# Moving operands 256 bytes behind the stationary ones, and gates built from 2-byte tables two tokens at a time

## The chip, the cores and the metric

The kernel runs on one core of one Trainium2 chip. The metric is the device time of one execution in microseconds (us). Before the change it is 2248.18 us, the median of 3 runs (2247.75 to 2248.98).

## The reference, cut to what matters

256 tokens of width 1024 pass through two blocks. The first is a gated MLP with a spatial mix, then attention with a sliding window. The second is retention, then latent attention, and behind each of these two stands a PEER layer. All matrix products are float32. The PEER layer is where the second half of the change works:

```python
def peer_ffn(x, w_q, sub_keys, u, v):
    ...
        s1, i1 = lax.top_k(s[:, :, 0], PEER_TOPK)
        s2, i2 = lax.top_k(s[:, :, 1], PEER_TOPK)
        ...
        top_s, pos = lax.top_k(cand_s, PEER_TOPK)
        eidx = jnp.take_along_axis(cand_i, pos, axis=-1)
        gate = jax.nn.softmax(top_s, axis=-1).astype(xb.dtype)
        h = jax.nn.gelu(jnp.einsum('thkd,td->thk', u[eidx], xb), approximate=False)
        return jnp.einsum('thk,thkd->td', gate * h, v[eidx])
```

Each token picks 8 heads x 16 experts out of 128 x 128 = 16384, and each picked expert is one neuron with a row of u, a row of v and a gate.

## The kernel before

A float32 product is made of three products of a rounded type (fp32r). ScalarE rounds an operand to its high part (line 155), VectorE subtracts to get the low part (line 156), and TensorE adds up high x high, high x low and low x high (lines 164, 165, 166). Weights come in units of 128 x 1024 floats (512 KB, `unit`, line 118), each cut into two pieces of 512 columns, `wh` and `wl`.

There are two ways to multiply. In `o2` (line 271) the weight piece is the stationary operand (128 columns at a time) and the tokens `xh`, `xl` are the moving one, 256 columns wide; one unit is 24 matmuls. It serves the gates of the MLP, of the attention and of retention, part of the queries, and the 128 units of u in each PEER layer. In `o1_unit` and `out_unit` the tokens are stationary and 512 columns of weights move; one unit of v is 12 matmuls.

Where the operands lie in a partition of SBUF: `front` begins with a pad of `X_PAD` floats (lines 37 and 52), then come `xh` and `xl`; the tile of `eps` is drawn out to `EPS_ROOM` floats (lines 36 and 57), so that what follows begins at a chosen place within 512 bytes. In this layout every `wh` and `wl` begins 160 bytes behind a multiple of 512, and `xh` and `xl` begin 352 bytes behind one: the moving operand of an `o2` matmul begins 192 bytes behind the stationary one, counted within 512. `apart` (line 175) does the same for the other token tiles that move (`xg`, `cqT`, `ckT`), with `APART` floats. In a unit of v the weights move and the other operand (`wdh`, `wdl`) also begins at 160, so there the distance is 0. Where the tokens `xh` are stationary and weights move (line 164 with `mm<-wh,xh`), it is 160 - 352, that is 320 within 512.

The PEER layer does not gather rows. It computes h for all 16384 experts (`u_block`, 128 units), multiplies it with a gate that is zero for the experts that were not picked, and runs all of v (`v_block`, 128 units). The gates come 8 tokens (`NT`) and 64 blocks of experts (`nb`) at a time from `gates` (line 1186): a one-hot `a` of 128 columns for each of the 128 picks of a token (its second index), a one-hot `e` of 64 columns (its first index), `b` as `e` times the high and the low part of the gate's weight, and two matmuls of 64 columns for each token, `a` stationary, `b` moving: 16 matmuls. VectorE compares `iota` (float32) with a table of indices (float32). For 6 of 8 groups ScalarE makes `a` instead, with one Square for each token and one Relu for four tokens (lines 1198 and 1199). The gate is multiplied into h in place by one instruction on VectorE that reads PSUM (line 1148).

Two passes of 32 gates run in each layer, woven (`weave`, line 104) one gate to two units: pass 1 between the last 64 units of u, pass 2 between the first 62 units of v. Behind pass 2 come the other units of v without gates. Each engine works through its own queue in the order that the program gives.

Of the kernel before, what the change touches and what calls it, by code (L numbers as in the profile page):

```python
# [10 lines left out]
F32 = mybir.dt.float32  # L11
F32R = mybir.dt.float32r
F16 = mybir.dt.float16
BF16 = mybir.dt.bfloat16
I32 = mybir.dt.int32
U32 = mybir.dt.uint32
AF = mybir.ActivationFunctionType
ALU = mybir.AluOpType
# [12 lines left out]
NPEER = 2  # L31
NBEGIN = 3
U2 = 64
PASSES = ((0, 64, 64, 6), (64, 64, 62, 6))
NT = 8
LINE = 512
EPS_ROOM = 48
X_PAD = 56
APART = 48
END_PAD = 80  # L40
GSCALE = 2.0 ** 15

# [1 line left out]
class Net:  # L44
    def __init__(s, ctx, tc, aps):
# [10 lines left out]
        s.cp = ctx.enter_context(tc.tile_pool(name="consts", bufs=1))  # L56
        s.eps = s.cp.tile([128, EPS_ROOM], F32, name="eps")[:, 0:1]

# [116 lines left out]
    def apart(pool, shapes):  # L175

        pool.tile([128, APART], F32, name="gap")
        tiles = [pool.tile(shape, F32R, name=name) for shape, name in shapes]
# [901 lines left out]
    def peer(s, i, outs, begin):  # L1080
        nc, d = s.nc, s.d
        with ExitStack() as es:


            p = pw = es.enter_context(s.pool(f"pw{i}", "right"))
            s.more_weights(es, f"wp{i}", 0, NPEER, "right")
            pg = es.enter_context(s.pool(f"pg{i}"))
            X = (s.xh, s.xl)
            tabs = [pw.tile([128, 256], F32, name=f"tab{j}") for j in range(2)]
            tabs.append(pw.tile([128, 2, 256], F16, name="tabg"))  # L1090
            hst = [es.enter_context(s.pool(f"ph{i}")).tile([128, 64, 256], F32, name="h0")]

            routing = ExitStack()
            skv = routing.enter_context(s.pool(f"ps{i}", "right")).tile([128, 2048], F32, name="sk")
            with s.urgent():
                nc.sync.dma_start(skv, d[f"p_sk{i}"])
            pk = routing.enter_context(s.pool(f"pk{i}", "right"))
            scratch = pk.tile([128, 2, 28 * 128], F32, name="scratch")
            q4 = pk.tile([128, 2, 512], F32, name="q4")
            si = pk.tile([128, 2, 2, 16, 16], F32, name="si")  # L1100
            rest = pk.tile([128, 256], F32, name="rest")
            s16 = [si[:, t, 0] for t in range(2)]
            i16 = [si[:, t, 1].bitcast(U32) for t in range(2)]

            def row(b):
                return hst[b // 64][:, b % 64, :]

            def u_block(b):
                hp = s.mm("acc")
                s.o2(s.unit(d[f"p_u{i}"][b]), 0, KB, X, hp[:, :256])  # L1110
                nc.scalar.activation(row(b), hp[:, :256], AF.Gelu)  # L1111

            qs = {}

            def q_unit(c):
                if c < 4:
                    qp = s.transposes(lambda j: q4[:, j, c * 128:c * 128 + 128], 2)
                else:
                    qp = s.mm()
                    s.o2(s.unit(d[f"p_q{i}"][c]), 0, KB, X, qp[:, :256])  # L1120
                qs[c] = p.tile([128, 256], F32, name="qT", tag="wd", bufs=6)
                nc.scalar.copy(qs[c], qp[:, :256])

            def s_unit(c):
                qT, sk = qs.pop(c), skv[:, c * 128:c * 128 + 128]
                sc = s.mm()
                for tt in range(2):
                    o = sc[:, tt * 128:tt * 128 + 128]
                    nc.tensor.matmul(o, qT[:, tt * 128:tt * 128 + 128], sk, start=True, stop=True)
                ss = p.tile([128, 256], F32, name="ss", tag="wd", bufs=6)  # L1130
                nc.scalar.copy(ss, sc[:, :256])
                for tt in range(2):
                    s.top16(rest[:, tt * 128:tt * 128 + 128], s16[tt][:, c, :], i16[tt][:, c, :],
                            ss[:, tt * 128:tt * 128 + 128])

            def v_in(b):
                wh = p.tile([128, 256], F32R, name="wdh", tag="wd", bufs=6)
                wl = p.tile([128, 256], F32R, name="wdl", tag="wd", bufs=6)
                s.split(wh, wl, row(b))
                return wh, wl  # L1140

            def v_block(b):
                s.out_unit(acc, s.unit(d[f"p_v{i}"][b]), v_in(b), False, False)

            def gate(t0, b0, nb, act):
                gp = s.gates(pg, t0, b0, nb, tabs, t0 // NT * act % 8 < act)
                hv = hst[b0 // 64][:, b0 % 64:b0 % 64 + nb, t0:t0 + NT].rearrange("p b t -> p t b")
                nc.vector.scalar_tensor_tensor(hv, gp[:, :NT * nb].rearrange("p (t b) -> p t b", b=nb),  # L1148
                                               1.0 / (GSCALE * ALPHA), hv,
                                               op0=ALU.mult, op1=ALU.mult)  # L1150

            for tt in range(2):
                nc.scalar.copy(q4[:, tt, :], outs[tt])
            for c in range(16):
                q_unit(c)
                u_block(c)
                s_unit(c)
            steps = []
            for tt in range(2):
                i16f = si[:, tt, 1]  # L1160
                nc.vector.tensor_copy(i16f, i16[tt])
                g = s.route(s16[tt], i16f, scratch[:, tt])
                steps += [lambda g=g: next(g)] * 16
            steps.append(lambda: s.gate_tables(scratch, tabs))
            s.weave([lambda b=b: u_block(b) for b in range(16, U2)], steps)
            routing.close()
            hst.append(es.enter_context(s.pool(f"pv{i}", "right")).tile([128, 64, 256], F32, name="h1"))
            blocks = [lambda b=b: u_block(b) for b in range(U2, 128)]
            for b0, nb, n, act in PASSES:
                s.weave(blocks[:n], [lambda t=t: gate(t, b0, nb, act) for t in range(0, 256, NT)])  # L1170
                blocks = blocks[n:]
                if b0 == 0:
                    for f in blocks:
                        f()
                    acc = s.accs()
                    s.skip_path(acc)
                    blocks = [lambda b=b: v_block(b) for b in range(125)]
            s.warm(hst[1][:, 63, 0:1])
            for f in blocks:
                f()  # L1180
            s.finish(acc, [d[f"p_v{i}"][b] for b in (125, 126, 127)], [v_in(b) for b in (125, 126, 127)])
            room = [hst[1][:, 36 + 4 * j:40 + 4 * j, :].rearrange("p b t -> p (b t)") for j in range(4)]

            return s.hand_over(s.post_ln(room, acc, d["ln_ffn_g"][i], d["ln_ffn_b"][i]), begin)

    def gates(s, p, t0, b0, nb, tabs, act):

        nc = s.nc
        i1t, i2t, gt = tabs
        sl = slice(t0, t0 + NT)  # L1190
        a = p.tile([128, NT, 128], F16, name="ga", tag="ga", bufs=2)
        if act:

            for j0 in range(0, NT, 4):
                q = p.tile([128, 4, 128], BF16, name="gq", tag="gq", bufs=1)
                for j in range(4):
                    t = t0 + j0 + j
                    nc.scalar.activation(q[:, j, :], s.iota, AF.Square, scale=-1.0, bias=i2t[:, t:t + 1])  # L1198
                nc.scalar.activation(a[:, j0:j0 + 4, :], q, AF.Relu, scale=-1.0, bias=1.0)  # L1199
        else:  # L1200
            nc.vector.tensor_tensor(a, s.iota[:, None, :].to_broadcast([128, NT, 128]),
                                    i2t[:, sl, None].to_broadcast([128, NT, 128]), op=ALU.is_equal)
        e = p.tile([128, NT, nb], F16, name="ge1", tag="g3", bufs=2)
        nc.vector.tensor_tensor(e, s.iota[:, None, b0:b0 + nb].to_broadcast([128, NT, nb]),  # L1204
                                i1t[:, sl, None].to_broadcast([128, NT, nb]), op=ALU.is_equal)
        b = p.tile([128, 2, NT, nb], F16, name="gb", tag="g2", bufs=2)
        nc.vector.tensor_tensor(b, e[:, None].to_broadcast([128, 2, NT, nb]),  # L1207
                                gt[:, :, sl, None].to_broadcast([128, 2, NT, nb]), op=ALU.mult)
        gp = s.mm()
        for j in range(NT):  # L1210
            for k in range(2):
                nc.tensor.matmul(gp[:, j * nb:(j + 1) * nb], a[:, j, :], b[:, k, j, :], start=k == 0, stop=k == 1)  # L1212
        return gp


# [97 lines left out]
```

## Time and profile before

| what | value |
|---|---|
| median of 3 runs | 2248.18 us |
| the profiled execution | 2246.99 us |
| its span, first to last instruction | 2245.3 us |
| TensorE, share of the span with a matmul in flight | 98% |
| VectorE | 83% |
| ScalarE | 68% |
| DMA, mean busy share | 53% |

TensorE's row counts a matmul as busy until its modelled end, and the next one begins long before that. So 98% does not say that TensorE runs at its best pace; the pace is read from the starts of successive matmuls in the timeline. The shares are means over stages with different limits: in the units of v without gates VectorE is a third idle, in pass 2 it is busy all the time.

### The profile page before, as it was taken

How to read it: one execution, taken by the hardware profiler on the slowest of the kernel's cores; microseconds unless marked ns; L12 is line 12 of the kernel's file. 1: busy time of each engine (PE TensorE's matmuls, PEld its weight loads, DVE VectorE, ACT ScalarE, POOL GpSimd, SP SyncE). 2: the span in 40 equal slices, each digit the busy share in tenths (PEclk: the TensorE clock that was granted, in tenths of full speed). 3: DMA queues.
4: the chain of work that ended last, by engine and by line, in shares of the span. 5: the costliest groups of instructions: out<-in, count | busy, mean ns of one | idle time of the engine just before them, and what ended most of it. 6: DMA issues, size and time to landing. Idle time of an engine off the chain costs nothing.

```text
span 2245.3 us, 43044 instructions
## 1 busy us (share of the span) xinstructions
PE 2207.5 (98%) x15726; PEld 1970.1 (88%) x15726; DVE 1871.7 (83%) x3685; ACT 1530.0 (68%) x3404; POOL 6.6 (0%) x15
## 2 busy tenths in 40 slices
PE   9999999999999999999999999999999999999998
PEld 7998878898999999987788888899999998777887
DVE  6967877567899899999986666689989999999666
ACT  5545865565555799888875556555569898887554
POOL 0000000000000000000000000000000000000000
PEclk9999999999999999999999999999999999999999
DMA  8555345453555655544565654355565554445664
GB/s 307 200 179 181 124 160 169 137 183 117 180 174 174 196 178 178 178 154 161 168 213 194 214 173 150 113 177 171 176 202 174 175 178 159 165 166 183 195 213 142
DMA packets 109223, 394.55 MB, mean 176 GB/s; under 512 B 12881, under 2 KB 13521, under 8 KB 108242
## 3 DMA queue, kind: packets, MB, share of 16 engines
q1 hardware_dynamic: 109010, 391.80, 53.1%
q8 instruction: 123, 2.02, 0.4%
q14 instruction: 90, 0.74, 0.1%
HBM read 390.70 MB, written 1.05 MB: 174 GB/s over the span
## 4 chain that ended last, share of the span: by engine, by line
PE 79%; DVE 13%; ACT 3%; issue 3%; DMA 2%; DVEq 0%; SPq 0%; ACTq 0%
PE mm L164 14%; PE mm L166 14%; PE mm L165 14%; PE acc L166 10%; PE acc L164 10%; PE acc L165 10%; DVE wl L156 4%; PE mm L1212 2%; DVE gb L1207 2%; DVE h L1148 1%; PE mm L194 1%; ACT wh L155 1%; DMA w<-in_p_u 1%; ACT gq L1198 1%; DVE ge L1204 1%
## 5 line engine op out<-in xcount | busy, mean ns | idle before, releaser
L155 ACT CAST wh<-w 128x512 fp32r<-128x512 f32 x1427 | 869.3, 614 | 530.2 <-PE mm L165 159.6
L156 DVE TENSOR_TENSOR wl<-w,wh 128x512 fp32r<-128x512 f32 x1427 | 960.4, 683 | 270.8 <-ACT wh L155 257.5
L164 PE MATMUL mm<-xh,wh 128*128 128x256 f32 x2624 | 737.2, 281 | 1.0 <-ACT h L1111 1.0
L166 PE MATMUL mm<-xh,wl 128*128 128x256 f32 x2624 | 729.6, 278 | 2.3 <-DVE wl L156 1.9
L165 PE MATMUL mm<-xl,wh 128*128 128x256 f32 x2624 | 728.3, 278 | 0.0
L166 PEld LDWEIGHTS mm<-xh,wl 128*128 128x128 f32 x2624 | 494.2, 188 | 4.9 <-DVE wl L156 4.7
L164 PEld LDWEIGHTS mm<-xh,wh 128*128 128x128 f32 x2624 | 493.0, 188 | 3.1 <-ACT h L1111 1.4
L165 PEld LDWEIGHTS mm<-xl,wh 128*128 128x128 f32 x2624 | 493.9, 188 | 1.5 <-issue 0.5
L166 PE MATMUL acc<-wh,wdl 128*128 128x512 f32 x1024 | 401.2, 392 | 7.9 <-DVE wdl L156 7.9
L164 PE MATMUL acc<-wh,wdh 128*128 128x512 f32 x1024 | 405.9, 396 | 0.0
L165 PE MATMUL acc<-wl,wdh 128*128 128x512 f32 x1024 | 399.2, 390 | 0.0
L1198 ACT ACTIVATE gq<-iota,tab 128x128 bf16<-128x128 f32 x768 | 267.7, 393 | 5.1 <-DVE tab L1060 1.6
L166 PEld LDWEIGHTS acc<-wh,wdl 128*128 128x128 f32 x1024 | 192.6, 188 | 54.4 <-DVE wdl L156 13.1
L165 PEld LDWEIGHTS acc<-wl,wdh 128*128 128x128 f32 x1024 | 193.0, 188 | 38.6
L164 PEld LDWEIGHTS acc<-wh,wdh 128*128 128x128 f32 x1024 | 192.7, 188 | 36.9
L1148 DVE SCALAR_TENSOR_TENSOR h<-mm,h 128x512 f32<-128x512 f32 x128 | 171.4, 1339 | 0.0
L1207 DVE TENSOR_TENSOR gb<-ge,tabg 128x1024 f16<-128x1024 f16 x128 | 155.5, 1215 | 0.0
L155 ACT CAST wdh<-h 128x256 fp32r<-128x256 f32 x256 | 102.7, 403 | 66.5 <-PE acc L165 57.4
L156 DVE TENSOR_TENSOR wdl<-h,wdh 128x256 fp32r<-128x256 f32 x256 | 106.9, 418 | 24.7 <-ACT wdh L155 24.2
L1199 ACT ACTIVATE ga<-gq 128x512 f16<-128x512 bf16 x192 | 120.3, 626 | 2.7
L164 PE MATMUL mm<-wh,xh 128*128 128x512 f32 (+1 forms) x272 | 110.3, 406 | 0.3 <-ACT xh L155 0.2
L166 PE MATMUL mm<-wh,xl 128*128 128x512 f32 (+1 forms) x272 | 105.7, 389 | 0.4 <-DVE xl L156 0.3
(352 smaller groups left out, 2293.5 us busy)
## 6 DMA issues: line engine op xcount, KB each, us to landing
w<-in_p_u SPq DMA_DIRECT2D x256, 512.0 KB, 3.6
w<-in_p_v SPq DMA_DIRECT2D x256, 512.0 KB, 4.2
w<-in_p_q SPq DMA_DIRECT2D x32, 512.0 KB, 3.5
w<-in_a_v SPq DMA_DIRECT2D x16, 512.0 KB, 5.4
w<-in_a_g SPq DMA_DIRECT2D x16, 512.0 KB, 3.6
w<-in_a_u SPq DMA_DIRECT2D x16, 512.0 KB, 3.7
w<-in_a_out SPq DMA_DIRECT2D x16, 512.0 KB, 3.5
w<-in_r_qk SPq DMA_DIRECT2D x16, 512.0 KB, 3.6
```

The source lines that it names most:

```text
L155: s.nc.scalar.copy(hi, src)
L156: s.nc.vector.tensor_tensor(lo, src, hi.bitcast(F32), op=ALU.subtract)
L164: s.nc.tensor.matmul(out, a[0], b[0], start=start, stop=False)
L165: s.nc.tensor.matmul(out, a[0], b[1], start=False, stop=False)
L166: s.nc.tensor.matmul(out, a[1], b[0], start=False, stop=stop)
L194: s.nc.tensor.transpose(p[:, j * 128:(j + 1) * 128], src(j), s.ident)
L1148: nc.vector.scalar_tensor_tensor(hv, gp[:, :NT * nb].rearrange("p (t b) -> p t b", b=nb), 1.0 / (GSCALE * ALPHA), hv, op0=ALU.mult, op1=AL ...
L1198: nc.scalar.activation(q[:, j, :], s.iota, AF.Square, scale=-1.0, bias=i2t[:, t:t + 1])
L1199: nc.scalar.activation(a[:, j0:j0 + 4, :], q, AF.Relu, scale=-1.0, bias=1.0)
L1204: nc.vector.tensor_tensor(e, s.iota[:, None, b0:b0 + nb].to_broadcast([128, NT, nb]), i1t[:, sl, None].to_broadcast([128, NT, nb]), op=ALU ...
L1207: nc.vector.tensor_tensor(b, e[:, None].to_broadcast([128, 2, NT, nb]), gt[:, :, sl, None].to_broadcast([128, 2, NT, nb]), op=ALU.mult)
L1212: nc.tensor.matmul(gp[:, j * nb:(j + 1) * nb], a[:, j, :], b[:, k, j, :], start=k == 0, stop=k == 1)
```

## The change

The first part moves token tiles by 64 bytes: `X_PAD` 56 to 72, `EPS_ROOM` 48 to 32 and `APART` 48 to 64. The sum of the first two is kept, so everything behind stays in its place within 512 bytes. `xh` and `xl` then begin at 416 within 512, 256 behind the weight pieces; where they are stationary the distance is 256 too.

The second part makes the tables of indices float16, adds `iota2` (every column number twice in a row, float16, copied by GpSimd once in a layer), and lays out the one-hots with two tokens side by side: the innermost dimension of every operand of the comparisons and of the products is now two float16 next to each other. `b` is made by two instructions in place of one. ScalarE's share of `a` goes, VectorE makes all of it. The matmuls read every second float16 of `a` and `b`. The multiplication into h runs with tokens innermost: h and the result are read and written in runs of 8 floats, PSUM with a step of 64 floats.

```diff
-PASSES = ((0, 64, 64, 6), (64, 64, 62, 6))
+PASSES = ((0, 64, 64), (64, 64, 62))
-EPS_ROOM = 48
-X_PAD = 56
-APART = 48
+EPS_ROOM = 32
+X_PAD = 72
+APART = 64
...
-            tabs = [pw.tile([128, 256], F32, name=f"tab{j}") for j in range(2)]
+            tabs = [pw.tile([128, 256], F16, name=f"tab{j}") for j in range(2)]
             tabs.append(pw.tile([128, 2, 256], F16, name="tabg"))
+            iota2 = pw.tile([128, 128, 2], F16, name="iota2")
+            for j in range(2):
+                nc.gpsimd.tensor_copy(iota2[:, :, j], s.iota)
+            tabs.append(iota2)
...
-            def gate(t0, b0, nb, act):
-                gp = s.gates(pg, t0, b0, nb, tabs, t0 // NT * act % 8 < act)
-                hv = hst[b0 // 64][:, b0 % 64:b0 % 64 + nb, t0:t0 + NT].rearrange("p b t -> p t b")
-                nc.vector.scalar_tensor_tensor(hv, gp[:, :NT * nb].rearrange("p (t b) -> p t b", b=nb),
+            def gate(t0, b0, nb):
+                gp = s.gates(pg, t0, b0, nb, tabs)
+                hv = hst[b0 // 64][:, b0 % 64:b0 % 64 + nb, t0:t0 + NT]
+                nc.vector.scalar_tensor_tensor(hv, gp[:, :NT * nb].rearrange("p (t b) -> p b t", b=nb),
                                                1.0 / (GSCALE * ALPHA), hv,
                                                op0=ALU.mult, op1=ALU.mult)
...
-        a = p.tile([128, NT, 128], F16, name="ga", tag="ga", bufs=2)
-        if act:
-            for j0 in range(0, NT, 4):
-                q = p.tile([128, 4, 128], BF16, name="gq", tag="gq", bufs=1)
-                for j in range(4):
-                    t = t0 + j0 + j
-                    nc.scalar.activation(q[:, j, :], s.iota, AF.Square, scale=-1.0, bias=i2t[:, t:t + 1])
-                nc.scalar.activation(a[:, j0:j0 + 4, :], q, AF.Relu, scale=-1.0, bias=1.0)
-        else:
-            nc.vector.tensor_tensor(a, s.iota[:, None, :].to_broadcast([128, NT, 128]),
-                                    i2t[:, sl, None].to_broadcast([128, NT, 128]), op=ALU.is_equal)
-        e = p.tile([128, NT, nb], F16, name="ge1", tag="g3", bufs=2)
-        nc.vector.tensor_tensor(e, s.iota[:, None, b0:b0 + nb].to_broadcast([128, NT, nb]),
-                                i1t[:, sl, None].to_broadcast([128, NT, nb]), op=ALU.is_equal)
-        b = p.tile([128, 2, NT, nb], F16, name="gb", tag="g2", bufs=2)
-        nc.vector.tensor_tensor(b, e[:, None].to_broadcast([128, 2, NT, nb]),
-                                gt[:, :, sl, None].to_broadcast([128, 2, NT, nb]), op=ALU.mult)
+        def hits(out, c0, n, at):
+            nc.vector.tensor_tensor(out, iota2[:, None, c0:c0 + n].to_broadcast([128, h, n, 2]),
+                                    at[:, sl].rearrange("p (q j) -> p q j", j=2)[:, :, None]
+                                    .to_broadcast([128, h, n, 2]), op=ALU.is_equal)
+        a = p.tile([128, h, 128, 2], F16, name="ga", tag="ga", bufs=2)
+        hits(a, 0, 128, i2t)
+        e = p.tile([128, h, nb, 2], F16, name="ge1", tag="g3", bufs=2)
+        hits(e, b0, nb, i1t)
+        b = p.tile([128, 2, h, nb, 2], F16, name="gb", tag="g2", bufs=2)
+        for k in range(2):
+            nc.vector.tensor_tensor(b[:, k], e, gt[:, k, sl].rearrange("p (q j) -> p q j", j=2)[:, :, None]
+                                    .to_broadcast([128, h, nb, 2]), op=ALU.mult)
         gp = s.mm()
         for j in range(NT):
             for k in range(2):
-                nc.tensor.matmul(gp[:, j * nb:(j + 1) * nb], a[:, j, :], b[:, k, j, :], start=k == 0, stop=k == 1)
+                nc.tensor.matmul(gp[:, j * nb:(j + 1) * nb], a[:, j // 2, :, j % 2], b[:, k, j // 2, :, j % 2],
+                                 start=k == 0, stop=k == 1)
```

## Rows read from the trace of the kernel before

**Rows 1.** Page, part 1: busy time, share of the span, instructions of each engine.

```profile
PE 2207.5 (98%) x15726; PEld 1970.1 (88%) x15726; DVE 1871.7 (83%) x3685; ACT 1530.0 (68%) x3404; POOL 6.6 (0%) x15
```

**Rows 2.** Busy time by engine in a stretch of pass 1 and one of pass 2.

```profile
core 0: us, PE busy (x) PEld busy (x) DVE busy (x) ACT busy (x) POOL busy (x), PEclk, DMA share, GB/s
800.00:850.00 50.00, 50.00 (x542) 49.68 (x541) 47.87 (x62) 45.52 (x115) 0.00 (x0) 1.00 0.55 177
1000.00:1050.00 50.00, 49.28 (x329) 39.31 (x328) 50.00 (x75) 43.79 (x107) 0.00 (x0) 1.00 0.50 164
```

**Rows 3.** TensorE's groups, shapes apart: out<-moving,stationary, shape, xcount | busy us, mean ns.

```profile
L164 PE MATMUL mm<-xh,wh 128*128 128x256 f32 x2624 | 737.2, 281 | 1.0 <-ACT h L1111 1.0
L164 PE MATMUL mm<-wh,xh 128*128 128x512 f32 x256 | 105.7, 413 | 0.3 <-ACT xh L155 0.2
L1212 PE MATMUL mm<-gb,ga 128*128 128x64 f16 x2048 | 82.3, 194 | 1.3 <-DVE gb L1207 1.2
```

**Rows 4.** TensorE's timeline, first PEER layer, distance 192: start us, us, what.

```profile
619.75 0.28 PE L164 MATMUL mm<-xh,wh 128*128 128x256 f32 x1
...
621.40 0.28 PE L166 MATMUL mm<-xh,wl 128*128 128x256 f32 x1
...
622.66 0.28 PE L164 MATMUL mm<-xh,wh 128*128 128x256 f32 x1
...
625.95 0.28 PE L166 MATMUL mm<-xh,wl 128*128 128x256 f32 x1
```

**Rows 5.** TensorE's timeline at two other distances: 320 (attention's kv), then 0 (v).

```profile
217.75 0.28 PE L165 MATMUL mm<-wl,xh 128*128 128x256 f32 x1
...
222.10 0.28 PE L166 MATMUL mm<-wh,xl 128*128 128x256 f32 x1
...
1199.72 0.39 PE L164 MATMUL acc<-wh,wdh 128*128 128x512 f32 x1
...
1202.90 0.39 PE L166 MATMUL acc<-wh,wdl 128*128 128x512 f32 x1
```

**Rows 6.** TensorE's timeline, pass 2 of the first layer: gates that follow undisturbed, and a stall.

```profile
978.93 0.64 PE L1212 MATMUL mm<-gb,ga 128*128 128x64 f16 x16
...
991.02 0.64 PE L1212 MATMUL mm<-gb,ga 128*128 128x64 f16 x16
...
1090.73 0.39 PE L165 MATMUL acc<-wl,wdh 128*128 128x512 f32 x1
1093.15 0.55 PE L166 MATMUL acc<-wh,wdl 128*128 128x512 f32 x1 [2.04 <-DVE wdl L156]
...
1096.90 0.39 PE L166 MATMUL acc<-wh,wdl 128*128 128x512 f32 x1
```

**Rows 7.** The gates' matmuls in pass 2 of each layer: min/median/max ns, first and last start.

```profile
L1212 PE MATMUL mm<-gb,ga x512: 193/193/204, 960.8 to 1149.2; 128*128 128x64 f16 x171
L1212 PE MATMUL mm<-gb,ga x512: 193/193/203, 1869.8 to 2057.9; 128*128 128x64 f16 x171
```

**Rows 8.** VectorE's groups, shapes apart, xcount | busy us, mean ns of one.

```profile
L156 DVE TENSOR_TENSOR wl<-w,wh 128x512 fp32r<-128x512 f32 x1403 | 948.4, 686 | 265.3 <-ACT wh L155 252.1 <-PE mm L165 0.6
L1148 DVE SCALAR_TENSOR_TENSOR h<-mm,h 128x512 f32<-128x512 f32 x128 | 171.4, 1339 | 0.0
L1207 DVE TENSOR_TENSOR gb<-ge,tabg 128x1024 f16<-128x1024 f16 x128 | 155.5, 1215 | 0.0
L156 DVE TENSOR_TENSOR wdl<-h,wdh 128x256 fp32r<-128x256 f32 x256 | 106.9, 418 | 24.7 <-ACT wdh L155 24.2 <-PE acc L164 0.4
L1204 DVE TENSOR_TENSOR ge<-iota,tab 128x512 f16<-128x512 f32 x128 | 87.2, 682 | 0.0
L1201 DVE TENSOR_TENSOR ga<-iota,tab 128x1024 f16<-128x1024 f32 x32 | 38.9, 1215 | 0.0
...
L339 DVE SCALAR_TENSOR_TENSOR h<-acc,lnmv,h 128x512 f32<-128x512 f32 x8 | 5.8, 741 | 0.1
```

**Rows 9.** ScalarE's groups that make a one-hot, in the same columns.

```profile
L1198 ACT ACTIVATE gq<-iota,tab 128x128 bf16<-128x128 f32 x768 | 267.7, 393 | 5.1 <-DVE tab L1060 1.6
L1199 ACT ACTIVATE ga<-gq 128x512 f16<-128x512 bf16 x192 | 120.3, 626 | 2.7
```

More of the change, by code (lines that the diff above doesn't have):

```diff
@@ L1168, in peer @@
             blocks = [lambda b=b: u_block(b) for b in range(U2, 128)]
-            for b0, nb, n, act in PASSES:
-                s.weave(blocks[:n], [lambda t=t: gate(t, b0, nb, act) for t in range(0, 256, NT)])
+            for b0, nb, n in PASSES:
+                s.weave(blocks[:n], [lambda t=t: gate(t, b0, nb) for t in range(0, 256, NT)])
                 blocks = blocks[n:]
@@ L1184, in peer, with gates @@
             return s.hand_over(s.post_ln(room, acc, d["ln_ffn_g"][i], d["ln_ffn_b"][i]), begin)
-    def gates(s, p, t0, b0, nb, tabs, act):
+    def gates(s, p, t0, b0, nb, tabs):
         nc = s.nc
-        i1t, i2t, gt = tabs
+        i1t, i2t, gt, iota2 = tabs
+        h = NT // 2
         sl = slice(t0, t0 + NT)
-        a = p.tile([128, NT, 128], F16, name="ga", tag="ga", bufs=2)
-        if act:
-            for j0 in range(0, NT, 4):
-                q = p.tile([128, 4, 128], BF16, name="gq", tag="gq", bufs=1)
-                for j in range(4):
-                    t = t0 + j0 + j
-                    nc.scalar.activation(q[:, j, :], s.iota, AF.Square, scale=-1.0, bias=i2t[:, t:t + 1])
-                nc.scalar.activation(a[:, j0:j0 + 4, :], q, AF.Relu, scale=-1.0, bias=1.0)
-        else:
-            nc.vector.tensor_tensor(a, s.iota[:, None, :].to_broadcast([128, NT, 128]),
-                                    i2t[:, sl, None].to_broadcast([128, NT, 128]), op=ALU.is_equal)
-        e = p.tile([128, NT, nb], F16, name="ge1", tag="g3", bufs=2)
-        nc.vector.tensor_tensor(e, s.iota[:, None, b0:b0 + nb].to_broadcast([128, NT, nb]),
-                                i1t[:, sl, None].to_broadcast([128, NT, nb]), op=ALU.is_equal)
-        b = p.tile([128, 2, NT, nb], F16, name="gb", tag="g2", bufs=2)
-        nc.vector.tensor_tensor(b, e[:, None].to_broadcast([128, 2, NT, nb]),
-                                gt[:, :, sl, None].to_broadcast([128, 2, NT, nb]), op=ALU.mult)
+        def hits(out, c0, n, at):
[10 more added lines that the diff above has]
+                                    .to_broadcast([128, h, nb, 2]), op=ALU.mult)
         gp = s.mm()
```

## The prediction

> **What bounds the kernel now.** I read the page's busy times first. TensorE has a matmul in flight 98% of the span, VectorE works 83%, ScalarE 68% [rows 1]. So the question is the pace of TensorE: where its matmuls follow each other more slowly than they can, and who makes it wait. For that I read the starts in its timeline, form by form, and then the stages.
>
> The matmuls of 256 columns are the largest form: three groups of 2624, of which one row stands for all [rows 3]. Their starts show two paces. In one stretch the 15 matmuls from 619.75 to 621.40 are 1.65 / 14 = 0.118 us apart. Just behind, the 30 from 622.66 to 625.95 are 3.29 / 29 = 0.1134 us apart [rows 4]. Same line, same tiles, same granted clock. I went through the whole timeline by this measure: about 1950 of some 7900 steps are at the upper pace (nearly all of the MLP's and retention's gates, and every second group of two units in the first 90 us of each PEER layer), the others at the lower. The upper pace costs 1950 x 0.0044 = 8.6 us in all.
>
> The stages say where another engine counts. In pass 1 TensorE is full and VectorE nearly so: 47.87 of 50 us. In pass 2 VectorE works all of its 50 us, ScalarE 43.79, and TensorE has gaps [rows 2]. One such gap: from 1090.73 to 1093.15 TensorE waits for a low part `wdl` that VectorE has yet to make. Behind it the 9 steps from 1093.15 to 1096.90 take 3.75 / 9 = 0.417 us where 0.227 is usual: the clock was granted at its lower level, 1.2 GHz, for as long [rows 5, 6].
>
> What these gaps cost I take from the gates in pass 2. Undisturbed, two steps from gate to gate take 991.02 - 978.93 = 12.09, so 6.045 us each [rows 6]. A pass has 31 steps; 60 units of v lie in them, so 29 steps hold two units and 2 hold one, which is shorter by 12 x 0.2271 = 2.73 us [rows 5]. That makes 29 x 6.045 + 2 x 3.32 = 181.9 us. The gates' first and last starts give 188.4 and 188.1 us; less 0.44 us for the last gate's own 16 matmuls that is 188.0 and 187.7 [rows 7]. So pass 2 loses 6.1 + 5.8 = 11.9 us in the two layers.
>
> **The change, part one: the distance.** No instruction is added or removed. What changes is the distance of the moving operand, 192 to 256 within 512 bytes, in some 8200 matmuls of 256 columns, and 320 to 256 in 816 of 512 columns (one of their groups is in [rows 3]). No row shows 256. The nearest ones: at 192 there are both paces [rows 4]; at 320 the 38 matmuls from 217.75 to 222.10 stand at 4.35 / 37 = 0.1176, all at the upper pace; at 0 the 15 of 512 columns from 1199.72 to 1202.90 stand at 3.18 / 14 = 0.2271, twice 0.1136, which is the lower pace [rows 5]. So the lower pace is what TensorE keeps without a disturbance, and I see no reason for a pace below it. The bounds: all at the lower pace, -8.6 us, with some 2 us more from the 816 wide ones, where their starts lie about 0.003 us above those of v; or all at the upper pace, (7900 - 1950) x 0.0044 = +26 us. 256 lies halfway between 192, mostly good, and 320, all bad, but at 320 the sample is one stretch of 48 matmuls, and long stretches at 192 are all bad as well. I take the mixture of today, 0, and keep -10.6 and +26 for the range.
>
> The Trainium skill (SBUF — State Buffer, Who interferes with whom) gives TensorE two independent read ports, one for the moving operand and one for weight loads, and says that it never waits on anyone. By that, the distance would be worth nothing, and the sum would be the same. The two paces of one form in rows 4 do not fit that as it stands, so I give the distance its own bounds.
>
> **Part two, on VectorE.** For one gate of pass 2 and two units of v, VectorE now does, by its rows [rows 8]: a quarter of `a` (32 of 128 gates), 0.30; `e` 0.68; `b` 1.215; the product into h 1.34; together 3.54. The two units add 4 x 0.686 + 2 x 0.418 = 3.58. That is 7.12 us of durations for a step of 6.045 in which VectorE never idles [rows 2]: neighbours overlap by about 1.07 us for 9.3 instructions, 0.115 each.
>
> Afterwards: `a` on every gate (1024 elements), `e` (512), two halves of `b` (512 each), the product. No row shows a comparison that makes two elements at a time. If it does, 1024 elements cost what 512 cost now, 0.68, and 512 what 256 cost, 0.418: 0.68 + 3 x 0.418 = 1.93. If it does not, 1.215 + 3 x 0.68 = 3.26. The row of `b` is no proof against: its operands are 2-byte already, yet 1024 elements take 1.215, but its innermost step over the weights is 0, and the change makes just that step 1. I take 1.93. The product into h now writes with a step of 1 KB and takes 1.34; the same instruction with contiguous operands, PSUM as its input and as many elements takes 0.74 (line 339) [rows 8]. Afterwards the side in SBUF is in runs and the side in PSUM is stepped: between 0.74 and 1.34, no reason for less, and more only if the stepped PSUM is the costly side. So a gate costs 2.67 to 3.27, and a step 6.25 to 6.85 less 11 x 0.115 = 1.27 for overlap: 5.0 to 5.6 us, under the 6.045 of TensorE. VectorE is no longer late, and I let all of the 11.9 us go, the slow clock behind the long gap included. What is next late is TensorE itself.
>
> The Trainium skill (VectorE: DVE Perf Modes, What auto-detection actually checks) has a two-source operation take two elements a cycle when every tensor is 16-bit with step 1. No run here shows it yet. By its slope, 1024 elements would be 1024 / 2 / 0.96 GHz = 0.53 us plus a fixed part, an estimate which is no further from 0.68 than that part.
>
> In pass 1, TensorE is full already; what VectorE saves there is worth nothing. The cover to name: at the dear end (3.26 + 1.34) pass 1 would have 4 x 0.686 + 4.6 - 9 x 0.115 = 6.3 us on VectorE for 6.02 us of TensorE.
>
> **Part two, the rest.** ScalarE loses 267.7 + 120.3 = 388 us [rows 9], all of it in the passes, where it is not the late engine; its casts come earlier and that only helps. GpSimd's two copies in each layer run about 190 us ahead of the first gate with nothing behind them: nothing. The first gate of each pass 1 waits for VectorE behind the tables now (`e` and `b`, 1.9 us) and will wait for `a`, `e` and `b`, 1.93 us: nothing. No DMA is moved.
>
> The gates' 2048 matmuls now read every second 2-byte element. Sixteen take 0.64 us to the modelled end of the last, which itself lasts 0.194 [rows 3, 6]: 0.03 us each. A step of 4 bytes is what the fp32r operands have, and they move 256 columns in 0.1134, so 64 in 0.028 [rows 4]: the moving side fits. The stationary side, 128 columns stepped, has no row; its far bound is the pace at which 4-byte weights are loaded one after another, 0.1134, so +0.083 x 2048 = +170 us. I take 0, the nearest row being the gates' own.
>
> **Sum.** Against the profiled execution of 2246.99 (span 2245.3 and 1.7 around it): 0 - 11.9 = 2235.1. The median of the runs is 1.2 above that execution, so 2236.3.
>
> **Rivals.**
> 1. *The distance settles at the lower pace everywhere.* For: at distance 0 it does. Against: nothing shows it for 256. 2236 - 10.6 = 2226.
> 2. *The distance settles at the upper pace everywhere*, slower than before. For: 320 shows nothing else. Against: 192 mostly keeps the lower. Its price is 0.0044 us for each matmul that changes over, and it outweighs part two from some 2700 of them on: 2236 + 26 = 2262.
> 3. *Two elements at a time do not happen*; VectorE stays the late engine. A step of pass 2 is then 3.26 + 0.74 to 1.34 + 3.58 - 1.27 = 6.3 to 6.9 us against 6.045: +16 to +55 in 64 steps, and 0 to +18 in pass 1: 2252 to 2309. Against: all operands are 2-byte with step 1 afterwards.
> 4. *Stepped weights load more slowly.* It decides from 6 ns for each of the 2048 matmuls on; twice the 0.03 of today gives +61, 2297.
> 5. *The gaps of pass 2 stay* because another wait takes the place of VectorE's: about 2247. Against: in the units of v without gates TensorE keeps 0.227 for hundreds of matmuls, so weights arrive in time.
>
> **Chances.** Forecast 0.40, rival 1 0.25, rival 2 0.14, rival 3 0.06, rival 4 0.05, rival 5 0.10. About 0.2% (4.5 us) is what a measurement can tell from no change. Faster: forecast, rival 1 and a little of rival 5, 0.66; same: 0.11; slower: 0.23. The range reaches from a little below rival 1 to rival 2: 2219 to 2263; outside lie rivals 3 and 4 in the main, and a pace below the lower one.
>
> **What would show it.** In the timeline of the new kernel: the share of steps of 256 columns at 0.118 and at 0.113 (part one, any third pace included). The rows of `ga` and `ge` at 0.68 and 0.42, or at 1.2 and 0.68. The row of the product into h between 0.74 and 1.34. Gates in pass 2 every 6.05 us without a longer step, VectorE idle there for a tenth or more, no stretch at the lower clock. Sixteen matmuls of a gate in 0.64 us. The prediction is wrong if the gates' matmuls or the matmuls of 256 columns keep a pace that no row here shows.

## The result and the profile after

The changed kernel takes 2265.81 us (median of 4 runs, 2263.58 to 2268.66) against 2247.97 (2247.24 to 2248.98) of the kernel before beside it: 1.0078 times as long, 95% interval 1.0066 to 1.0091. The forecast was 2236, with a range of 2219 to 2263. The profiled execution took 2266.74 us, with a span of 2265.0.

The page's busy times (as [rows 1]):

```profile
PE 2239.8 (99%) x15726; PEld 2013.6 (89%) x15726; DVE 1767.2 (78%) x3909; ACT 1225.6 (54%) x2444; POOL 8.9 (0%) x19
```

Two stretches of 50 us, the first in pass 1 and the second in pass 2 (columns as in [rows 2]):

```profile
800.00:850.00 50.00, 50.00 (x509) 49.66 (x508) 38.48 (x73) 24.38 (x48) 0.00 (x0) 1.00 0.52 166
1010.00:1060.00 50.00, 50.00 (x330) 40.64 (x329) 46.18 (x93) 25.48 (x49) 0.00 (x0) 1.00 0.58 178
```

VectorE and ScalarE are relieved as forecast: in pass 1 VectorE falls from 47.87 to 38.48 us of 50, in pass 2 from 50 to 46.18, and TensorE has no gap in pass 2 any more. Yet in the 50 us of pass 1 TensorE begins 509 matmuls where it began 542 [rows 2]. Not one of the busy shares tells of a loss; the count of matmuls does.

The starts say why. TensorE's timeline of the changed kernel, in the first PEER layer (as [rows 4]), then the gates' matmuls in pass 1, where two gates have 48 matmuls of 256 columns between them:

```profile
624.75 0.28 PE L164 MATMUL mm<-xh,wh 128*128 128x256 f32 x1
...
627.51 0.28 PE L166 MATMUL mm<-xh,wl 128*128 128x256 f32 x1
...
823.34 0.65 PE L1217 MATMUL mm<-gb,ga 128*128 128x64 f16 x16
...
829.66 0.65 PE L1217 MATMUL mm<-gb,ga 128*128 128x64 f16 x16
```

The 24 matmuls from 624.75 to 627.51 are 2.76 / 23 = 0.1200 us apart: a third pace, slower than both of [rows 4]. Over the whole trace 7284 of the 7741 steps between matmuls that move `xh` and `xl` stand at it. From gate to gate pass 1 takes 829.66 - 823.34 = 6.32 us. In the kernel before it was 6.02 (the second row is three gates behind the first):

```profile
818.29 0.64 PE L1212 MATMUL mm<-gb,ga 128*128 128x64 f16 x16
...
836.35 0.64 PE L1212 MATMUL mm<-gb,ga 128*128 128x64 f16 x16
```

that is (836.35 - 818.29) / 3 = 6.02. Each layer has 31 such steps: 31 x 0.30 = 9.3 us lost in pass 1.

Pass 2 went the other way. The gates' matmuls in it, first layer, then second (columns as in [rows 7]):

```profile
L1217 PE MATMUL mm<-gb,ga x512: 191/193/203, 978.5 to 1160.5; 128*128 128x64 f16 x171
L1217 PE MATMUL mm<-gb,ga x512: 191/193/203, 1895.7 to 2077.7; 128*128 128x64 f16 x171
```

182.0 us each, where it was 188.4 and 188.1 [rows 7]: 6.4 + 6.1 = 12.5 us won. Put together by stages (from the starts in the two timelines): the units of u ahead of pass 1 lost 5.5 and 5.8 us, pass 1 lost 9.3 twice, the MLP's gates 1.6, the start 1.8; the rest of the PEER layers, with pass 2 in it, won 6.9 and 6.6. That is 33.3 - 13.5 = 19.8 us, and the spans differ by 19.7.

VectorE's and TensorE's groups that answer to [rows 3] and [rows 8]:

```profile
L156 DVE TENSOR_TENSOR wl<-w,wh 128x512 fp32r<-128x512 f32 x1403 | 962.0, 689 | 371.7 <-ACT wh L155 357.5 <-PE mm L165 0.6
L164 PE MATMUL mm<-xh,wh 128*128 128x256 f32 x2624 | 751.2, 286 | 0.0
L1212 DVE TENSOR_TENSOR gb<-ge,tabg 128x512 f16<-128x512 f16 x256 | 107.0, 421 | 0.0
L1153 DVE SCALAR_TENSOR_TENSOR h<-mm,h 128x512 f32<-128x512 f32 x128 | 87.6, 684 | 0.0
L1202 DVE TENSOR_TENSOR ga<-iota,tab 128x1024 f16<-128x1024 f16 x128 | 87.5, 684 | 0.0
L1217 PE MATMUL mm<-gb,ga 128*128 128x64 f16 x2048 | 83.7, 193 | 0.0
L1202 DVE TENSOR_TENSOR ge<-iota,tab 128x512 f16<-128x512 f16 x128 | 53.9, 422 | 2.1
```

### The profile page after: what moved, and what is told of

Same layout as the page of the kernel before. It is cut to its first block, busy times and chain, and to the rows that moved or that the text cites. A ratio compares the mean times of both kernels' runs of the same rounds, so it can differ in the third digit from the quotient of the medians.

```text
span 2265.0 us, 42382 instructions
## 1 busy us (share of the span) xinstructions
PE 2239.8 (99%) x15726; PEld 2013.6 (89%) x15726; DVE 1767.2 (78%) x3909; ACT 1225.6 (54%) x2444; POOL 8.9 (0%) x19
## 4 chain that ended last, share of the span: by engine, by line
PE 96%; DVE 2%; ACT 1%; DMA 1%; issue 0%; SPq 0%; DVEq 0%; ACTq 0%
PE mm L164 17%; PE mm L165 17%; PE mm L166 17%; PE acc L164 12%; PE acc L166 12%; PE acc L165 12%; PE mm L1217 3%; PE mm L194 1%; PE mm L1134 1%; PE mm L763 1%; DVE wl L156 1%; PE mm L552 0%; ACT wh L155 0%; PE mm L424 0%; PE mm L948 0%
## 5 line engine op out<-in xcount | busy, mean ns | idle before, releaser
L156 DVE TENSOR_TENSOR wl<-w,wh 128x512 fp32r<-128x512 f32 x1427 | 974.0, 687 | 375.5 <-ACT wh L155 361.2
L164 PE MATMUL mm<-xh,wh 128*128 128x256 f32 x2624 | 751.2, 286 | 0.0
L165 PE MATMUL mm<-xl,wh 128*128 128x256 f32 x2624 | 742.4, 283 | 0.0
L166 PE MATMUL mm<-xh,wl 128*128 128x256 f32 x2624 | 742.3, 283 | 0.0
L165 PEld LDWEIGHTS mm<-xl,wh 128*128 128x128 f32 x2624 | 503.5, 192 | 1.5 <-issue 0.5
L164 PEld LDWEIGHTS mm<-xh,wh 128*128 128x128 f32 x2624 | 503.1, 192 | 1.7 <-issue 0.2
L1212 DVE TENSOR_TENSOR gb<-ge,tabg 128x512 f16<-128x512 f16 x256 | 107.0, 421 | 0.0
L165 PE MATMUL mm<-wl,xh 128*128 128x512 f32 (+1 forms) x272 | 105.0, 387 | 0.2 <-DVE wl L156 0.2
L1116 ACT ACTIVATE h<-mm 128x256 f32<-128x256 f32 x256 | 96.9, 378 | 0.6 <-DVE tabg L1065 0.5
L1153 DVE SCALAR_TENSOR_TENSOR h<-mm,h 128x512 f32<-128x512 f32 x128 | 87.6, 684 | 0.0
```

The source lines that it names most:

```text
L156: s.nc.vector.tensor_tensor(lo, src, hi.bitcast(F32), op=ALU.subtract)
L164: s.nc.tensor.matmul(out, a[0], b[0], start=start, stop=False)
L165: s.nc.tensor.matmul(out, a[0], b[1], start=False, stop=False)
L166: s.nc.tensor.matmul(out, a[1], b[0], start=False, stop=stop)
L1212: nc.vector.tensor_tensor(b[:, k], e, gt[:, k, sl].rearrange("p (q j) -> p q j", j=2)[:, :, None] .to_broadcast([128, h, nb, 2]), op=ALU.mult)
```

## The experiments

The theory after the result: the third pace comes from the distance of 256 bytes alone, and the gates by themselves bring what was forecast. The rival: the new gates slow TensorE (2-byte traffic of VectorE, or stepped operands), also between the gates. In all that follows "pace" is the step from start to start of matmuls of 256 columns. A kernel for which the text gives a ratio was executed 4 to 12 times, every other one once.

### The gates alone

```diff
-EPS_ROOM = 32
-X_PAD = 72
-APART = 64
+EPS_ROOM = 48
+X_PAD = 56
+APART = 48
```

(from the changed kernel: its gates, the old distance of 192)

> The changed kernel with the distance put back to 192 (EPS_ROOM 48, X_PAD 56, APART 48), so part two alone. Theory: the loss comes from the distance alone, by a third pace of 0.120 us for matmuls of 256 columns, and part two gives what was forecast. Then paces of 0.113 and 0.118 as before, pass 1 steps of 6.02 us, pass 2 of 6.03 without a longer one, and 2248 - 13 = 2235 us (2231 to 2238). Rival: the new gates (stepped operands, more 2-byte traffic of VectorE) bring the third pace, whatever the distance; then 0.120 stays and the time is near 2265.

2246.59 us, ratio 0.9990 (0.9982 to 0.9999). The third pace is gone and pass 2 is as good as in the changed kernel, so the distance is to blame for the third pace. But nearly the whole gain of pass 2 is eaten by pass 1. Two gates and a stretch between them in this kernel's timeline:

```profile
818.61 0.66 PE L1217 MATMUL mm<-gb,ga 128*128 128x64 f16 x16
...
822.72 0.28 PE L164 MATMUL mm<-xh,wh 128*128 128x256 f32 x1
...
824.72 0.28 PE L166 MATMUL mm<-xh,wl 128*128 128x256 f32 x1
824.85 0.66 PE L1217 MATMUL mm<-gb,ga 128*128 128x64 f16 x16
```

The 18 matmuls are 2.00 / 17 = 0.1176 apart, the upper pace, and a gate's step is 6.24 instead of 6.02. In pass 1 of the kernel before nearly all were at the lower pace. So there are two effects, and the rival is right about one of them.

### The distance alone

The kernel before with the first three lines of the change, and nothing of the gates.

```diff
-EPS_ROOM = 48
-X_PAD = 56
-APART = 48
+EPS_ROOM = 32
+X_PAD = 72
+APART = 64
```

> The kernel before with the distance of 256 and the old gates, so part one alone. Theory (distance alone): all matmuls of 256 columns at 0.120, pass 1 steps of 6.33, and pass 2 keeps its gaps: 2248 + 32 = 2280 us (2274 to 2288). Rival (the gates bring the pace): 0.113 and 0.118 as before and 2248.

2276.61 us beside 2249.67 of the kernel before, ratio 1.0119 (1.0102 to 1.0136), 6961 steps at 0.120, gaps in pass 2 as before (188.5 us from the first to the last start of its gates' matmuls in the first layer, where it was 188.4). With the old gates pass 1 has steps of 6.3 us too:

```profile
821.71 0.64 PE L1212 MATMUL mm<-gb,ga 128*128 128x64 f16 x16
828.01 0.64 PE L1212 MATMUL mm<-gb,ga 128*128 128x64 f16 x16
834.32 0.64 PE L1212 MATMUL mm<-gb,ga 128*128 128x64 f16 x16
```

The distance alone costs 26.9 us, about what was held possible if all steps went to the upper pace, but by a pace beyond it.

### Only the stepped one-hots

The distance of 192; one-hots two by two and read with a step by TensorE, but float32 tables, ScalarE's share and the old product into h.

```diff
-        a = p.tile([128, NT, 128], F16, name="ga", tag="ga", bufs=2)
+        a = p.tile([128, h, 128, 2], F16, name="ga", tag="ga", bufs=2)
...
-                nc.tensor.matmul(gp[:, j * nb:(j + 1) * nb], a[:, j, :], b[:, k, j, :], start=k == 0, stop=k == 1)
+                nc.tensor.matmul(gp[:, j * nb:(j + 1) * nb], a[:, j // 2, :, j % 2], b[:, k, j // 2, :, j % 2],
+                                 start=k == 0, stop=k == 1)
```

> Distance 192; the one-hots are laid out two tokens side by side and read stepped by TensorE as in the change, but made at the old cost: float32 tables, ScalarE's share of `a`, the old order of the product into h. If the stepped reading of TensorE is what leaves the units of u at the upper pace, pass 1 has steps of 6.23 us and 0.118 between matmuls of 256 columns, and its gates' matmuls are 0.031 apart. If it is the 2-byte traffic of VectorE, pass 1 keeps 6.02 and 0.1134. (VectorE may be late in pass 2 as before, or more: its cost there is not the question.)

2247.42 us, and pass 1 is at the upper pace as with all of the new gates:

```profile
821.07 0.66 PE L1216 MATMUL mm<-gb,ga 128*128 128x64 f16 x16
827.30 0.66 PE L1216 MATMUL mm<-gb,ga 128*128 128x64 f16 x16
```

VectorE's groups of the same kernel (as [rows 8]):

```profile
L1211 DVE TENSOR_TENSOR gb<-ge,tabg 128x512 f16<-128x512 f16 x256 | 98.6, 425 | 0.0
L1148 DVE SCALAR_TENSOR_TENSOR h<-mm,h 128x512 f32<-128x512 f32 x128 | 172.7, 1349 | 0.2
```

Neither VectorE's 2-byte comparisons nor ScalarE's absence is needed for it: the new layout, read with a step by TensorE, is enough. (ScalarE's stepped writes and the halves of `b` came with it and were not tried by themselves.) In this kernel pass 2 takes 182.1 and 182.0 us from the first to the last start of its gates' matmuls, as in the changed one: of all that VectorE saves there, `b` in two halves, 2 x 425 ns for 1215, already closes the gaps.

### Old gates in pass 1, new ones in pass 2

```diff
+                if b0:
+                    return gate2(t0, b0, nb)
```

(on the kernel before: `gate2` is the changed kernel's gate, with its own float16 tables; `e` has one buffer in place of two)

> Distance 192; pass 1 with the old gates (contiguous one-hots, ScalarE's share of `a`), pass 2 with the new ones. Theory: the gates-only kernel won 12 us in pass 2 and lost some 13 us in pass 1, where the new gates' matmuls leave the units of u behind them at the upper pace. Then pass 1 has steps of 6.02 us again, pass 2 steps of 6.03 without a gap, and the time is 2248 - 12 = 2236 us, 10 to 13 below the kernel before. Rival: the upper pace of pass 1 came from elsewhere (VectorE's tables, addresses of tiles); then pass 1 keeps 6.23 and the time stays near 2246.

2235.94 us (2232.88 to 2237.48), ratio 0.9942 (0.9929 to 0.9956): faster than both kernels. Two gates of pass 1, three steps apart:

```profile
818.37 0.64 PE L1227 MATMUL mm<-gb,ga 128*128 128x64 f16 x16
...
836.43 0.64 PE L1227 MATMUL mm<-gb,ga 128*128 128x64 f16 x16
```

18.06 / 3 = 6.02 us, and pass 2 runs at 6.03 without a gap. This is the forecast's sum come true, 2236, in a kernel that leaves out the two things that the forecast priced at nothing, the distance and the new gates ahead of units of u.

### Other distances, with the new gates

`X_PAD`, `EPS_ROOM` and `APART` only, so that all token tiles stand 0, 64, 128, 160, 224 or 320 bytes behind the weights.

> The changed kernel at distance 128 (X_PAD 40, EPS_ROOM 64, APART 32). If the pace grows steadily with the distance from 0 up to 256 (0.113 at 0 for 512 columns, 0.113 with some 0.118 at 192, 0.120 at 256), 128 is all at 0.113 and the time is 8 to 10 us under that of 192 with the same gates, some 2226. If the pace goes up and down with the distance within a shorter period (64 or 128 bytes), 128 and 256 are alike: 0.120 and 2265.

> The changed kernel at distance 0 (X_PAD 8, EPS_ROOM 96, APART 0). In v, 512 moving columns at distance 0 stand at the lower pace throughout. If that carries over to 256 columns: 0.1134 everywhere, pass 1 steps of 6.02, and 2248 - 12 - 8.6 - 2 = 2226 us. If with 256 columns the load of the next weights is what the pace hangs on, and not the moving side, 0 tells nothing and may be 0.118 to 0.120: 2245 to 2266 us.

> The new gates, all token tiles moved so that the distance is 64 bytes. Theory A, that the pace of 256 columns depends on the distance within 256 bytes (0 and 256 gave the same 0.120): then 64 equals 320, which stood at 0.1176 in the kernel before, so every step at 0.1176 and about 2246.6 + 2600 x 0.0044 = 2258 us. Theory B, that it depends on the distance within 512 bytes and 192 is the one good place of those in use: 64 lies between 0 (0.120) and 128 (0.119), so 0.119 to 0.120 and about 2263 to 2266 us.

> The new gates, distance 320 bytes. Theory A (only the distance within 256 counts): the same paces as the run at 64, step by step within 0.0005 us, and a time within 3 us of it. Theory B (within 512): 0.1176 everywhere as in the attention's stretch of the kernel before, 2258 us, while the run at 64 is at 0.119 or above.

> The new gates, distance 224 bytes, halfway between 192 (0.1133 and 0.1177) and 256 (0.120). If the pace grows steadily away from 192: 0.117 to 0.119, some 2255 us. If 192 is a narrow good place: 0.1195 to 0.120 everywhere, 2264 us. If the good place lies between 192 and 256: 0.1133 nearly everywhere, 2227 us, and then a better version of the kernel exists.

> The new gates, distance 160 bytes, halfway between 128 (0.119) and 192. If the pace grows steadily away from 192: 0.1165 to 0.118, some 2252 us. If 192 is a narrow good place: 0.1187 to 0.1195, 2262 us. If the good place lies between 128 and 192: 0.1133 nearly everywhere, 2227 us.

| distance | us | paces of 256 columns in the PEER layers | a step of pass 1 | mean pace, tokens stationary, 512 columns |
|---|---|---|---|---|
| 0 | 2265.85, ratio 1.0075 (1.0060 to 1.0091) | 0.120 | 6.33 | 0.2277 |
| 64 | 2245.83 | 0.1177 and 0.1133 | 6.23 and 6.02 in turn | 0.2333 |
| 128 | 2263.50, ratio 1.0061 (1.0044 to 1.0079) | 0.1185 to 0.120 | 6.27 and 6.34 in turn | 0.2326 |
| 160 | 2266.07 | 0.1172 to 0.119, then 0.120 | 6.34 | 0.2335 |
| 192 | 2246.59 | 0.1133 and 0.1177 | 6.23 | 0.2304 (0.2292 in the kernel before) |
| 224 | 2259.04 | 0.1183 | 6.26 | 0.2333 |
| 256 | 2265.81 | 0.120 | 6.33 | 0.2277 |
| 320 | 2245.75 | 0.1177 and 0.1133 | 6.23 and 6.02 in turn | 0.2334 |

The paces are means over undisturbed units of 24 matmuls. In the last column the weights move, so the distance counts the other way round there: 64 in the row of 192, 192 in the rows of 64 and 320. At distance 0 two gates of pass 1 are as far apart as at 256, 6.32 to 6.33 us:

```profile
821.80 0.65 PE L1218 MATMUL mm<-gb,ga 128*128 128x64 f16 x16
828.12 0.65 PE L1218 MATMUL mm<-gb,ga 128*128 128x64 f16 x16
```

The theory of a steady growth with the distance fell with 128 (2226 was expected). 0 behaves as 256, and 64 as 320, in every column: what counts is the distance within 256 bytes. A period of 128 would come near (64 and 192 are the good ones), but 128 is not 0 and 192 is not 64: their steps of pass 1 differ. Of the places tried only 64 and 192 reach the lower pace at all; between them and beyond them it is 0.117 to 0.120. Theory A of the runs at 64 and 320 has its equality, though neither its single pace of 0.1176, which came from one stretch, nor its 2258 us. Of 224 and 160 no one expectation fits both: 224 (2259.04) lies nearest to a steady growth away from 192, 160 (2266.07) to a narrow good place.

At 64 the two paces take turns, and so one can see where they part. Two gates of that kernel, with the two matmuls behind each:

```profile
823.07 0.65 PE L1217 MATMUL mm<-gb,ga 128*128 128x64 f16 x16
823.55 0.36 PE L164 MATMUL mm<-xh,wh 128*128 128x256 f32 x1
823.75 0.28 PE L165 MATMUL mm<-xl,wh 128*128 128x256 f32 x1
...
829.08 0.66 PE L1217 MATMUL mm<-gb,ga 128*128 128x64 f16 x16
829.57 0.36 PE L164 MATMUL mm<-xh,wh 128*128 128x256 f32 x1
829.78 0.28 PE L165 MATMUL mm<-xl,wh 128*128 128x256 f32 x1
```

Behind the first gate the 48 matmuls run at 0.1133 (6.01 us to the next gate), behind the second at 0.1177 (6.23). All that differs in time ahead of them is some 0.005 us: the gate's matmuls last a little longer, and the first start comes as much later. An obvious rival is that the double buffers of `a` and `b`, which also take turns, set the pace. The second layer of the same kernel speaks against it:

```profile
1675.22 0.66 PE L1217 MATMUL mm<-gb,ga 128*128 128x64 f16 x16
1681.45 0.66 PE L1217 MATMUL mm<-gb,ga 128*128 128x64 f16 x16
1687.68 0.65 PE L1217 MATMUL mm<-gb,ga 128*128 128x64 f16 x16
1693.70 0.66 PE L1217 MATMUL mm<-gb,ga 128*128 128x64 f16 x16
```

Here two slow steps (6.23 twice) stand at the beginning, and the first fast one (6.02) follows the third gate, while in the first layer, and in both layers of the same program at 320, the fast ones follow the second gate, the fourth and so on. The same buffers thus see either pace. What is shown is that a run of matmuls keeps one pace from its beginning to the next gate; that the 0.005 us choose it is not shown, they may as well be a trace of a state that TensorE carries over. That the stepped gates of pass 1, whose 16 matmuls take 0.66 instead of 0.64, lock the units behind them in this way is argued, not shown.

### One of the two operands moved

```diff
         s.xh = front.tile([128, KB, 256], F32R, name="xh")
+        front.tile([128, 16], F32, name="between")
         s.xl = front.tile([128, KB, 256], F32R, name="xl")
```

(new gates; `xh` at 192, `xl` at 256)

> The gates of the changed kernel, xh at distance 192 and xl at 256 (16 floats between the two tiles). Theory: what counts is where the moving operand of one matmul stands against the weights that are loaded while it moves, so the step that begins with xl (line 165) is 0.120 and the steps that begin with xh (lines 164 and 166) are 0.113 or 0.118: a mean of 0.1155 to 0.1185. Rival: the pace is a state of the whole chain, in which TensorE settles after a disturbance; then the steps of the three lines are equal, all 0.120 or all near 0.113.

2254.22 us. Neither expectation held. In pass 1 the mean paces of the three lines were 0.1176, 0.1196 and 0.1166, in the units of u ahead of it 0.1210, 0.1189 and 0.1177: the matmul with the moved operand is not alone in being slower. So the steps of the three lines hang together; which state that is, this one run does not tell.

### Distance or place

All runs so far moved the tokens. These two have the new gates again, and move the weights as well.

```diff
-X_PAD = 72
-END_PAD = 80
+X_PAD = 56
+END_PAD = 96
```

(from the changed kernel: tokens at 352, weights at 96, distance 256)

```diff
-EPS_ROOM = 32
-APART = 64
-END_PAD = 80
+EPS_ROOM = 48
+APART = 48
+END_PAD = 64
```

(from the changed kernel: tokens at 416, weights at 224, distance 192)

> The new gates. The token tiles stay where they were before the change (352 within 512) and all weights, with everything behind them, begin at 96 within 512 instead of 160, so that the distance is 256 as in the changed kernel, but both ends lie elsewhere within 256. If it is the distance that counts: 0.120 us for nearly every step of 256 columns, 6.33 us for a gate of pass 1 and 2265 us. If it is the place of the moving operand itself: as with the new gates at distance 192, paces of 0.1133 and 0.1177, 6.23 us, 2246 us.

> The new gates. The token tiles begin at 416 within 512 as in the changed kernel and all weights at 224, so that the distance is 192 as before the change. If it is the distance that counts: paces of 0.1133 and 0.1177, 6.23 us for a gate of pass 1 and 2246 us, as with the new gates alone. If it is the place of the moving operand: 0.120 everywhere and 2265 us.

2264.84 and 2243.20 us. Gates of pass 1, first of the one, then of the other:

```profile
821.22 0.65 PE L1217 MATMUL mm<-gb,ga 128*128 128x64 f16 x16
...
833.87 0.65 PE L1217 MATMUL mm<-gb,ga 128*128 128x64 f16 x16
```

```profile
817.88 0.66 PE L1217 MATMUL mm<-gb,ga 128*128 128x64 f16 x16
...
836.58 0.66 PE L1217 MATMUL mm<-gb,ga 128*128 128x64 f16 x16
```

12.65 / 2 = 6.33 and 18.70 / 3 = 6.23: the first has 7267 steps at 0.120, the second 18. It is the distance, wherever the two lie.

### Units of u in two halves of 128 tokens

To see what sets the pace at 256 columns: the load of 128 weight columns, or the columns that move. The changed kernel with

```diff
-                s.o2(s.unit(d[f"p_u{i}"][b]), 0, KB, X, hp[:, :256])
+                w = s.unit(d[f"p_u{i}"][b])
+                for t in range(2):
+                    c = slice(t * 128, t * 128 + 128)
+                    s.o2(w, 0, KB, [x[:, :, c] for x in X], hp[:, c])
```

> The changed kernel (distance 256) with each unit of u multiplied in two halves of 128 tokens: twice the matmuls, each of 128 columns. The moving side of one would take half of 0.113 to 0.120, so the step shows what one load of weights takes beside it. Theory: the load of 128 4-byte columns takes about as long as 256 moving columns, and it is what sets the pace: steps of 0.107 to 0.120 for 128 columns too, and a kernel longer by 6144 x 0.11 = 700 us. Rival: the load is hidden with much room and the moving side sets the pace: steps near 0.060, and a kernel about as long as the changed one.

3996.62 us. Its timeline in the first units of u, then three stretches of the same layer (columns as in [rows 2]):

```profile
581.60 0.27 PE L164 MATMUL mm<-xh,wh 128*128 128x128 f32 x1
...
583.94 0.28 PE L164 MATMUL mm<-xh,wh 128*128 128x128 f32 x1
```

```profile
560.00:660.00 100.00, 100.00 (x877) 100.00 (x877) 59.15 (x240) 38.92 (x83) 0.00 (x0) 1.00 0.37 122
700.00:800.00 100.00, 97.07 (x454) 96.50 (x453) 50.81 (x110) 17.14 (x34) 0.00 (x0) 0.50 0.20 63
1000.00:1100.00 100.00, 100.00 (x471) 100.00 (x470) 13.16 (x19) 14.57 (x29) 0.00 (x0) 0.50 0.15 49
```

From 581.60 to 583.94 are 21 steps of 2.34 / 21 = 0.111 us. Half the columns move, and the step is 0.111 instead of 0.120: what sets it is not the number of moving columns alone. The load of the next 128 4-byte columns is the nearest candidate, for every matmul here brings its own; but a matmul of 128 columns whose weights stay was not run, so that it is the load, and that a distance can disturb the pace because neither side has room, are inferences. The rest of the time, far beyond what was expected, is the clock, told below.

## Why the prediction was wrong, step by step

- *The distance, taken as 0 between -10.6 and +26: wrong.* Alone it cost 26.9 us. The step that failed is the pricing of 256 bytes with the two paces that the rows happen to show: the lower as what TensorE keeps "without a disturbance", the upper as the far bound, and today's mixture, 0, in between. In its place 256 gave a pace of its own, 0.120, slower than both, at 7284 of 7741 steps. Three things stood behind the error. Distance 0 was read from matmuls of 512 columns, twice 0.1136, as if half a wide step were a narrow one; at distance 0 the narrow ones stand at 0.120 and the wide ones are at their best. The pace at 320 was read from one stretch as "all bad"; at 320 both paces occur, as at 192. And 256 was placed between 192 and 320 on a line, where in fact the distance wraps round at 256: 256 is 0. The reservation at the end, that a third pace would upset it, was the right one to have and should have had a price: two paces gave no ground for taking the slower one as the last.
- *The rule of the Trainium skill* (SBUF — State Buffer, Who interferes with whom), that TensorE's two read ports are independent and that it never waits on anyone, was weighed in the prediction and gave the same sum. These runs speak against that use of it: the same instructions, with the full clock granted, take 0.1133, 0.1177 or 0.120 by the distance of two operands. Whether other engines' accesses delay TensorE was not tried, nor whether the ports are where the distance acts.
- *Rival 2, all at the upper pace, 2262:* nearest in time and in sign, by the wrong pace. It took part two at its full gain on top; so did the sum.
- *Pass 2, 11.9 us: right*, 12.5 measured, no gap, the clock granted in full, gates 6.03 us apart.
- *VectorE's gate, 2.67 to 3.27 us: mechanism right, size too dear.* `a` 0.684, `e` 0.422, halves of `b` 0.421: 1.93 forecast, 1.95 measured for `a`, `e` and `b`. By this the trace agrees with what the Trainium skill (VectorE: DVE Perf Modes, What auto-detection actually checks) says of 16-bit operands with step 1, and runs of two elements are enough for it. The product into h took 0.684, less than the lower end of 0.74, so the stepped side in SBUF, which is read and written in place, made all the difference to its former 1.34, and the stepped read of PSUM shows no cost. The sum is 2.63. The credit of 1.27 for overlap was too large: 2.63 and two units of v (4 x 0.689 + 2 x 0.42) are 6.23 us of durations, and 46.18 of 50 us busy is 5.57 of a step of 6.03, so some 0.7 is overlap. The two errors offset each other, and 5.57 lies within the forecast's 5.0 to 5.6, at its end; VectorE idles 8% there and not the tenth that was named.
- *Pass 1, "what VectorE saves there is worth nothing": right, but it was not all that moves there.* The 16 gate matmuls were looked at for their own time only, and that was nearly right (0.031 instead of 0.030 us apart, 2 us in all). What they do to the 48 matmuls behind them, 0.0044 x 48 = 0.21 us each time, 13 us over 62 steps, was not looked for, though the kernel before showed units of one form at two paces.
- *Rivals 3, 4 and 5* did not come: two elements at a time happen, the stepped stationary operand loads at 0.031 each, no other wait took the place in pass 2.

So of two effects that the forecast set at zero, one (the distance) makes the kernel slower, and the other cancels the gain of the gates at the old distance: 2246.59 instead of 2236. At the new distance the pace is at 0.120 anyway, so the second effect is hidden there, and the gates are worth most of what was forecast: the distance alone costs 26.9 us against the kernel before beside it, both together 17.8, a gain of 9.1 by these two comparisons (10.8 by the bare medians, 2276.61 and 2265.81) where 11.9 was forecast.

What stays open is the mechanism within TensorE: why 64 and 192 within 256 bytes allow the lower pace and 0, 128, 160 and 224 don't, and what puts a run of matmuls into one pace or the other.

## What to carry to other kernels

Where TensorE is full, count its matmuls for each stretch and read their start-to-start steps form by form; a busy share of 99% hid a loss of 5% in pass 1. Where each matmul of 256 columns brings its own load of 128 4-byte columns, try the distance between stationary and moving operand, in steps of 64 bytes within 256, and measure each form: the best place of the wide form (0) was among the worst of the narrow one. A price of zero for "the same instructions at another address", or for what an edit does to the instructions behind it, needs a bound of its own, beyond the paces that the trace happens to show.

## What the runs showed of the hardware beyond that

- The pace of fp32r matmuls depends on the distance of the two operands within 256 bytes, by up to 6% at 256 columns (0.1133 to 0.120) and 2.5% at 512 (0.2277 to 0.2335), with the wide form's best at 0.
- In the kernel with 128 columns the clock was granted in full through 100 us of gapless work from 560 to 660 (1.00), at steps of 0.111. A wait of 6.3 us from 693.19 on, for a low part that VectorE made late, brought the lower level of 1.2 GHz (0.50 in the second stretch above), and gapless work at 0.213 from 1000 to 1100 did not bring the full level back; it came back in the units of v with their 512 columns. In the kernel before, a wait of 2.04 us ahead of matmuls of 512 columns cost the lower level for about 4 us only [rows 6]. So after a gap the narrow form kept the slow clock for the whole stage, and in the second layer again (0.50 from 2500 to 3610).
- VectorE took 0.684 us for 512 float32 elements read from PSUM with a step of 256 bytes, and 1.34 for the same with a step of 1 KB on the side in SBUF [rows 8].
